# Three matmuls of 256 columns per weight tile in place of one of 512 and one of 256

## The chip, the cores and the metric

The kernel runs on one core of one Trainium2 chip. The metric is device time in microseconds (us) from start to end of one execution; the lower the better. The core has a matrix engine (TensorE, "PE" in the profile, its weight loads "PEld"), a vector engine (VectorE, "DVE"), a scalar engine (ScalarE, "ACT"), GpSimd ("POOL") and a sync engine ("SP") that here issues DMAs. TensorE writes to PSUM, an accumulation memory of eight banks; one bank holds 512 float32 values on each of 128 partitions. Everything else is kept in SBUF, the core's working memory.

## The reference

The reference is a small decoder trunk on 256 tokens of width 2048, with one gated-linear-attention layer and one block-sparse attention layer, each followed by a gated feed-forward layer with a convolution of width 3. Cut to what matters here:

```
h = x
h = h + gla_mixer(h)       # proj = rms_norm(h) @ w_in -> q, k, v, g ; ... ; o @ w_out
h = h + conv_ffn(h)        # a, u = split(conv3(rms_norm(h) @ w_up)); (silu(a) * u) @ w_down
h = h + moba_mixer(h)      # q, k, v projections, 16 heads; softmax; o @ w_out
h = h + conv_ffn(h)
```

All values are float32. FFN_HIDDEN is 5632, so each w_up is 2048 x 11264 and each w_down 5632 x 2048. Most of the work is products of the 256 tokens with these weight matrices.

## The kernel before

The kernel keeps the residual stream `h` feature-major: eight tiles of 128 partitions x (2 x 256), which hold two blocks of 128 features for all 256 tokens. A product whose result is feature-major takes a 128 x 128 tile of weights as the stationary operand and the tokens as the moving one.

The matmuls run in float32r, a type that keeps fewer bits than float32. To come close to float32, each operand is split into a high part (the value cast to float32r) and a low part (the rest). A product is then high x high + high x low + low x high; low x low is left out. The tokens' parts lie side by side in one tile: columns 0 to 255 hold the high part, 256 to 511 the low part.

`gemm` (line 222) makes one feature-major result of 2 x 128 features x 256 tokens over `kts` contraction tiles: 16 for a width of 2048, 44 for the down-projections. A step takes one half chunk of weights, 1024 columns, which is 4 contraction tiles x 2 feature blocks. For each of these eight weight tiles there are two matmuls. Line 233 multiplies the high weights with all 512 columns, so columns 0 to 255 of the result get high x high and 256 to 511 get high x low. Line 234 multiplies the low weights with the first 256 columns and adds that to columns 0 to 255. In the last step of a group all tiles of feature block 0 come before those of block 1. The result fills two banks, and the two halves are still to be added.

That addition is part of the evacuation. `both` (line 257) copies the right half to SBUF on ACT (line 259) and adds the left half on DVE (line 260). It is used for keys, queries, gates and the up-projections, and a multiplication by the token's norm scale follows (lines 395, 464, 479, 506). `residual` (line 266) adds the two halves to `h` one after the other on DVE (lines 267, 268). The last group of the kernel does the same for each feature block separately (lines 675, 676), and then sends the block out.

`gemm_tok` (line 238) makes token-major results (values, and the heads' queries and keys). Here the tokens are stationary and 512 columns of weights are moving; three matmuls (lines 248 to 250) add up in the same columns. The change doesn't touch it, but it shares the PSUM pool `acc_ps`, which has three buffers of two banks; two more banks, in the pool `mis_ps`, serve everything else.

Other runs of 256 columns are in `mix` (lines 316 to 318, three that add up in the same columns, and 319 with 128), in the gate logits (line 353), the scores (589) and the sums over partitions (196).

`WeightStream` loads the weights ahead by DMA and splits each half chunk of 1024 columns on ACT (line 77) and DVE (line 78), two steps ahead, into three buffers each of `whi` and `wlo`. The order of the instructions on each engine comes from a scheduler that works on the program as a whole; `after(n, job)` puts smaller jobs such as norms, scores and softmax between the steps of the big products. Values are scaled (lines 309, 310, 312) when the norm scale is there, the first of them ten steps behind their product.

Of the kernel before, what the change touches and what calls it, by code (L numbers as in the profile page):

```python
# [8 lines left out]
F32 = mybir.dt.float32  # L9
# [9 lines left out]
S = 256  # L19
# [15 lines left out]


class WeightStream:
    """Weights in the order of their use: loaded ahead, split ahead into float32r high and low parts."""

    AHEAD = 2  # L40

# [49 lines left out]
def trunk(ctx: ExitStack, tc: tile.TileContext, xT, cst, msk, w1p, w2a, w_k, w_qa, w_v, w_g, w_go,  # L91
# [7 lines left out]
    parts = ctx.enter_context(tc.tile_pool(name="parts", bufs=3))  # L99
    tmp = ctx.enter_context(tc.tile_pool(name="tmp", bufs=6))  # L100
    small = ctx.enter_context(tc.tile_pool(name="small", bufs=2))
    acc_ps = ctx.enter_context(tc.tile_pool(name="acc_ps", bufs=3, space=PSUM))
    mis_ps = ctx.enter_context(tc.tile_pool(name="mis_ps", bufs=2, space=PSUM))
    dram = ctx.enter_context(tc.tile_pool(name="dram", bufs=1, space=DRAM))

# [3 lines left out]
    def temp(name, shape=(128, 2, S), dt=F32):  # L109
        return tmp.tile(list(shape), dt, name=name, tag="temp")  # L110
# [78 lines left out]
        V.tensor_mul(dst, y, u)  # L189

    def spread_sum(ps, sq):
        """Sum over partitions on every partition; the operand goes in as its two float32r parts."""
        halves_ = temp("sum_parts", dt=F32R)
        split(halves_[:, 0], halves_[:, 1], sq)
        for i in range(2):
            T.matmul(ps, ones, halves_[:, i], start=i == 0, stop=i == 1)
# [25 lines left out]
        return halves_  # L222

    def gemm(xs, kts):
        ps = acc_ps.tile([128, 2, 512], F32, name="acc")
        for q0 in range(0, kts, 4):
            hi, lo = step()
            order = [(k, b) for k in range(4) for b in range(2)]
            for k, b in sorted(order, key=lambda kb: kb[1]) if q0 == kts - 4 else order:
                kt = q0 + k  # L230
                x = xs(kt)
                c = k * 256 + b * 128
                T.matmul(ps[:, b, :], hi[:, c:c + 128], x, start=kt == 0, stop=False)  # L233
                T.matmul(ps[:, b, :S], lo[:, c:c + 128], x[:, :S], start=False, stop=kt == kts - 1)  # L234
        ws.prefetch(cur[0])
        return ps

# [16 lines left out]
    def rows(xs):  # L254
        return lambda kt: xs[kt // 2][:, kt % 2, :]

    def both(ps, name):
        t = temp(name)
        A.copy(t, ps[:, :, S:])
        V.tensor_add(t, t, ps[:, :, :S])  # L260
        return t

    def bc(r):
        return r[:, None, :S].to_broadcast([128, 2, S])

    def residual(ps, p):
        V.tensor_add(h[p], h[p], ps[:, :, S:])
        V.tensor_add(h[p], h[p], ps[:, :, :S])

    def split(dst_hi, dst_lo, src):  # L270
        A.copy(dst_hi, src)
        V.tensor_sub(dst_lo, src, dst_hi.bitcast(F32))

    class Norm:
        """Takes the residual stream pair by pair: norm-weighted operand parts and the token scale."""

        def __init__(self, c, name, columns=False):
            self.c, self.name, self.columns, self.xs = c, name, columns, []
# [9 lines left out]
        def close(self):  # L288
            self.rstd = token_rstd(self.acc, self.columns)

    # GLA
    nrm = Norm(C_GN, "xw", True)
    for p in range(2):
        nrm.operand(p)
# [9 lines left out]
    vg = [(vg0[hd], vg1[hd // 2][:, hd % 2, :]) for hd in range(GH)]  # L304

    def v_out(v, ps, n):
        """Scales the values; the first token tile goes out as float32r parts, the second as it is."""
        r0, r1 = (n.rstd[:, S + t:S + t + 1] for t in range(2))
        A.activation(v[0][:, 0, :], ps[:, 0, :], AF.Copy, scale=r0)
        V.scalar_tensor_tensor(v[0][:, 1, :], ps[:, 0, :], r0, v[0][:, 0, :].bitcast(F32),  # L310
                               op0=OP.mult, op1=OP.subtract)
        A.activation(v[1], ps[:, 1, :], AF.Copy, scale=r1)
# [78 lines left out]
    for hd in range(GH):  # L391
        ps = gemm(xs, KT)
        rstd = nrm.rstd
        k = both(ps, "k")
        V.tensor_mul(k, k, bc(rstd))
        b = bcum[hd]
        d = small.tile([128, 2, 4], F32, name="dec", bufs=4)
        last = chunks(b)[:, :, :, 63:64]
        A.activation(d[:, :, :, None], last, AF.Exp)
        ke = slot([128, 2, 2, 2, 128], F32, "kie")  # L400
        qk = slot([128, 2, 2 * S], F32, "qq")
        eb = temp("eb")
        A.activation(eb, b, AF.Exp, scale=-1.0)
        V.tensor_mul(ke[:, :, :, 0, :], tiles(k), tiles(eb))
        A.copy(ke[:, :, :, 1, 64:], ke[:, :, :, 0, 64:])
        db = temp("db")
        V.tensor_sub(chunks(db), last.to_broadcast([128, 2, 4, 64]), chunks(b))
        A.activation(db, db, AF.Exp)
        V.tensor_mul(ke[:, :, :, 1, :64], tiles(k)[:, :, :, :64], tiles(db)[:, :, :, :64])
        V.tensor_mul(qk[:, :, 384:448], ke[:, :, 0, 1, :64], d[:, :, 1:2].to_broadcast([128, 2, 64]))  # L410
        V.tensor_mul(qk[:, :, 448:512], k[:, :, 64:128], db[:, :, 64:128])
        kie.append(ke)
        qq.append(qk)
        dec.append(d)
# [45 lines left out]

    for hd in range(GH):
        ps = gemm(xs, KT)
        q = both(ps, "q")
        V.scalar_tensor_tensor(q, q, 1.0 / 16.0, bc(rstd), op0=OP.mult, op1=OP.mult)
        eb = temp("eb")
        A.activation(eb, bcum[hd], AF.Exp)
        qk = qq[hd]
        V.tensor_mul(qk[:, :, :S], q, eb)
        A.copy(qk[:, :, 256:320], qk[:, :, 128:192])
        V.tensor_mul(qk[:, :, 320:384], qk[:, :, 192:256], dec[hd][:, :, 2:3].to_broadcast([128, 2, 64]))  # L470
        for lag, job in ((2, gla_scores), (4, gla_values), (6, gla_norm)):
            after(lag, lambda job=job, hd=hd: job(hd))

    go = []
    for hd in range(GH):
        for c in range(2):
            ps = gemm(xs, KT)
            g = both(ps, "g")
            V.tensor_mul(g, g, bc(rstd))
            A.activation(g, g, AF.Silu)  # L480
            V.tensor_mul(g, g, bc(heads[hd]["r"]))
            for i in range(2):
                V.scalar_tensor_tensor(g[:, i, :], heads[hd]["o"][:, 2 * c + i, :], col(C_ON + 2 * c + i),
                                       g[:, i, :], op0=OP.mult, op1=OP.mult)
            gx = slot([128, 2, 2 * S], F32R, "go")
            split(gx[:, :, :S], gx[:, :, S:], g)
            go.append(gx)
# [10 lines left out]
    def ffn(layer, nrm, then):  # L498
        xs = rows(nrm.xs)
        hid = []  # L500
        cw = C_CW + layer * 3 * 2 * FT
        cb = C_CB + layer * 2 * FT
        for j in range(FT):
            ps = gemm(xs, KT)
            t = both(ps, "up")
            V.tensor_mul(t, t, bc(nrm.rstd))  # L506
            au = temp("au")
            for i in range(2):
                n = i * FT + j
                A.activation(au[:, i, :], t[:, i, :], AF.Identity, bias=col(cb + n),  # L510
                             scale=col(cw + 2 * 2 * FT + n))
                V.scalar_tensor_tensor(au[:, i, 1:], t[:, i, :S - 1], col(cw + 2 * FT + n), au[:, i, 1:],  # L512
                                       op0=OP.mult, op1=OP.add)
                V.scalar_tensor_tensor(au[:, i, 2:], t[:, i, :S - 2], col(cw + n), au[:, i, 2:],  # L514
                                       op0=OP.mult, op1=OP.add)
            A.activation(au[:, 0, :], au[:, 0, :], AF.Silu)
            V.tensor_mul(au[:, 0, :], au[:, 0, :], au[:, 1, :])
            if j % 2 == 0:
                hid.append(slot([128, 2, 2 * S], F32R, "hid"))
            split(hid[-1][:, j % 2, :S], hid[-1][:, j % 2, S:], au[:, 0, :])  # L520
        then(rows(hid))
# [3 lines left out]
    n_q = Norm(C_MN, "xw", True)  # L525
    ffn(0, n_ffn, lambda xs: project(xs, FT, [n_q]))

    # cross-decoder: with S equal to the block, no block is fully past, and only the own block counts
    V.scalar_tensor_tensor(kqw, col(C_KN), 128.0 ** -0.5, col(C_QN), op0=OP.mult, op1=OP.mult)
    bias = []  # L530

# [32 lines left out]
        return t_  # L564

    def features(t_, c, f, scale, c0):
        """Turns two heads; queries or keys 0..127 stay whole, those from c0 on go out as float32r parts."""
        tp = bank("tr", (128, 2, S))
        for i in range(2):
            for t in range(2):  # L570
                T.transpose(tp[:, i, 128 * t:128 * t + 128],  # L571
                            t_[:, t, (2 * c + i) * 128:(2 * c + i + 1) * 128], ident)
        whole, halves_ = f[0][:, 2 * c:2 * c + 2, :], f[1][c]
        A.activation(whole, tp[:, :, :128], AF.Copy, scale=scale)
        hi, lo = halves_[:, :, 0, :], halves_[:, :, 1, :]
        A.activation(hi, tp[:, :, c0:], AF.Copy, scale=scale)
        V.scalar_tensor_tensor(lo, tp[:, :, c0:], scale, hi.bitcast(F32), op0=OP.mult, op1=OP.subtract)
# [89 lines left out]
    def last(xs):  # L667
        for p in range(NP):
# [3 lines left out]
                nc.sync.dma_start(out[p], h[p].rearrange("a b c -> a (b c)"))  # L672
                continue
            for i in range(2):
                V.tensor_add(h[p][:, i], h[p][:, i], ps[:, i, S:])
                V.tensor_add(h[p][:, i], h[p][:, i], ps[:, i, :S])
                (nc.sync, A)[i].dma_start(out[p, :, S * i:S * i + S], h[p][:, i])

    ffn(1, n_ffn, last)
# [86 lines left out]
```

## Time and profile before

| | |
|---|---|
| median of 3 runs | 2264.71 us (2260.82 to 2264.79) |
| profiled execution | 2262.2 us of span; the page gives no other time of it |
| instructions | 31304, of which 12514 matmuls and 12514 weight loads |
| PE busy | 2249.8 us (99%) |
| PEld busy | 1945.7 us (86%) |
| DVE busy | 1502.8 us (66%) |
| ACT busy | 1199.6 us (53%) |
| DMA | 420.17 MB, mean 186 GB/s |
| granted TensorE clock | 0.999 |

The span runs from the first to the last instruction of one execution. Busy time of an engine is the time in which at least one of its instructions runs; matmuls overlap in the records, so a TensorE that is 99% busy isn't at its peak, and the mean duration of a matmul is longer than the distance from its start to the next one's. Groups of instructions are listed as line, engine, operation, output<-inputs, shape and count, then busy time in us, mean duration in ns, and the idle time of the engine ahead of them with what ended it. Rows of the timeline begin with the start and the duration in us. The chain of waits is followed back from the last instruction, at each step to what released it.

### The profile page before, as it was taken

The numbers are of one execution on the slowest core, as the hardware profiler recorded it, in microseconds if no ns is written. First come the engines' busy times: TensorE is split into PE (matmuls) and PEld (weight loads), VectorE is DVE, ScalarE is ACT, GpSimd is POOL, SyncE is SP. The second block draws the span as 40 slices with busy tenths as digits, with TensorE's granted clock in tenths as the row PEclk, the third lists the DMA queues.
The fourth block names the chain that finished last, engine by engine and source line by source line (L and its number), as shares of the span: only waits on it lengthen the run. The fifth ranks groups of instructions, "written<-read, shape, count | busy, mean of one in ns | idle before, by whom it ended". The sixth has DMA issues, their size and how long they took to land.

```text
span 2262.2 us, 31304 instructions
## 1 busy us (share of the span) xinstructions
PE 2249.8 (99%) x12514; PEld 1945.7 (86%) x12514; DVE 1502.8 (66%) x2021; ACT 1199.6 (53%) x1667; POOL 25.0 (1%) x27
## 2 busy tenths in 40 slices
PE   8999999999999999999999999999999999999999
PEld 6889888888888888888888888888888888888887
DVE  6676776777777777555556666667777777764444
ACT  6555654655555555444456565556555555543332
POOL 0000000000000000000010000000000000000000
PEclk9999999999999999999999999999999999999999
DMA  6554455555555554555565544555555555555553
GB/s 243 186 186 142 170 185 186 188 195 194 187 186 189 193 195 178 186 199 190 197 219 181 179 168 149 186 186 187 186 186 186 187 186 187 186 183 190 196 205 122
DMA packets 62180, 420.17 MB, mean 186 GB/s; under 512 B 7073, under 2 KB 7857, under 8 KB 13138
## 3 DMA queue, kind: packets, MB, share of 16 engines
q1 hardware_dynamic: 61074, 415.82, 52.3%
q0 software_dynamic: 672, 2.17, 0.3%
q8 instruction: 98, 1.61, 0.3%
q14 instruction: 48, 0.39, 0.1%
q10 hardware_dynamic: 288, 0.18, 0.0%
HBM read 416.02 MB, written 2.12 MB: 185 GB/s over the span
## 4 chain that ended last, share of the span: by engine, by line
PE 99%; DVE 0%; DMA 0%; ACT 0%; SPq 0%; issue 0%
PE acc L233 54%; PE acc L234 27%; PE acc L249 5%; PE acc L250 5%; PE acc L248 5%; PE sT L431 0%; PE tr L571 0%; DMA h<-xT 0%; PE s L589 0%; PE pT L609 0%; DVE bcum L366 0%; PE z L339 0%; PE s L587 0%; PE o L319 0%; PE oT L319 0%; DVE wlo L78 0%
## 5 line engine op out<-in xcount | busy, mean ns | idle before, releaser
L78 DVE TENSOR_TENSOR wlo<-wraw,whi 128x1024 fp32r<-128x1024 f32 (+1 forms) x785 | 959.9, 1224 | 671.3 <-ACT whi L77 665.8
L77 ACT CAST whi<-wraw 128x1024 fp32r<-128x1024 f32 (+1 forms) x785 | 823.7, 1050 | 970.8 <-PE acc L233 744.7
L233 PE MATMUL acc<-xw,whi 128*128 128x512 f32 x3328 | 1166.6, 396 | 0.0
L234 PE MATMUL acc<-xw,wlo 128*128 128x256 f32 x3328 | 929.5, 279 | 0.0
L233 PEld LDWEIGHTS acc<-xw,whi 128*128 128x128 f32 x3328 | 624.7, 188 | 149.8
L234 PEld LDWEIGHTS acc<-xw,wlo 128*128 128x128 f32 x3328 | 627.0, 188 | 0.2
L233 PE MATMUL acc<-hid,whi 128*128 128x512 f32 x1408 | 492.9, 396 | 0.0
L234 PE MATMUL acc<-hid,wlo 128*128 128x256 f32 x1408 | 392.7, 279 | 0.0
L233 PEld LDWEIGHTS acc<-hid,whi 128*128 128x128 f32 x1408 | 264.3, 188 | 63.7
L234 PEld LDWEIGHTS acc<-hid,wlo 128*128 128x128 f32 x1408 | 265.2, 188 | 0.0
L248 PE MATMUL acc<-whi,xw 128*128 128x512 f32 x256 | 101.7, 397 | 6.8 <-ACT xw L166 4.9
L249 PE MATMUL acc<-wlo,xw 128*128 128x512 f32 x256 | 102.0, 398 | 1.0 <-DVE wlo L78 1.0
L250 PE MATMUL acc<-whi,xw 128*128 128x512 f32 x256 | 101.3, 396 | 0.0
L249 PE MATMUL acc<-wlo,xkv 128*128 128x512 f32 x256 | 100.6, 393 | 0.0
L248 PE MATMUL acc<-whi,xkv 128*128 128x512 f32 x256 | 100.5, 393 | 0.0
L250 PE MATMUL acc<-whi,xkv 128*128 128x512 f32 x256 | 100.4, 392 | 0.0
L510 ACT ACTIVATE au<-up,cs 128x256 f32<-128x256 f32 x176 | 95.8, 592 | 5.0 <-DVE up L506 5.0
L233 PE MATMUL acc<-go,whi 128*128 128x512 f32 x256 | 90.5, 399 | 0.0
L233 PE MATMUL acc<-ox,whi 128*128 128x512 f32 x256 | 89.1, 394 | 0.0
L512 DVE SCALAR_TENSOR_TENSOR au<-up,cs,au 128x255 f32<-128x255 f32 x176 | 76.9, 479 | 0.0
L514 DVE SCALAR_TENSOR_TENSOR au<-up,cs,au 128x254 f32<-128x254 f32 x176 | 76.7, 478 | 0.0
L234 PE MATMUL acc<-go,wlo 128*128 128x256 f32 x256 | 71.9, 281 | 0.0
(196 smaller groups left out, 1551.8 us busy)
## 6 DMA issues: line engine op xcount, KB each, us to landing
wraw<-w_up SPq DMA_DIRECT2D x176, 1024.0 KB, 4.7
wraw<-w_dn SPq DMA_DIRECT2D x80, 1024.0 KB, 4.8
wraw<-w_g SPq DMA_DIRECT2D x16, 1024.0 KB, 4.7
wraw<-w_go SPq DMA_DIRECT2D x16, 1024.0 KB, 4.7
wraw<-w_mq SPq DMA_DIRECT2D x16, 1024.0 KB, 4.8
wraw<-w_kk SPq DMA_DIRECT2D x16, 1024.0 KB, 4.7
wraw<-w_kv SPq DMA_DIRECT2D x16, 1024.0 KB, 4.7
wraw<-w_mo SPq DMA_DIRECT2D x16, 1024.0 KB, 4.8
```

The lines of the kernel that those rows point to most:

```text
L77: nc.scalar.copy(hi[:, a:b], src[:, a:b])
L78: nc.vector.tensor_sub(lo[:, a:b], src[:, a:b], hi[:, a:b].bitcast(F32))
L233: T.matmul(ps[:, b, :], hi[:, c:c + 128], x, start=kt == 0, stop=False)
L234: T.matmul(ps[:, b, :S], lo[:, c:c + 128], x[:, :S], start=False, stop=kt == kts - 1)
L248: T.matmul(ps[:, t, :], xh, wh, start=kt == 0, stop=False)
L249: T.matmul(ps[:, t, :], xh, wl, start=False, stop=False)
L250: T.matmul(ps[:, t, :], xl, wh, start=False, stop=kt == KT - 1)
L510: A.activation(au[:, i, :], t[:, i, :], AF.Identity, bias=col(cb + n), scale=col(cw + 2 * 2 * FT + n))
L512: V.scalar_tensor_tensor(au[:, i, 1:], t[:, i, :S - 1], col(cw + 2 * FT + n), au[:, i, 1:], op0=OP.mult, op1=OP.add)
L514: V.scalar_tensor_tensor(au[:, i, 2:], t[:, i, :S - 2], col(cw + n), au[:, i, 2:], op0=OP.mult, op1=OP.add)
```

## The change

Each weight tile now has three matmuls of 256 columns: high weights x high tokens, high weights x low tokens, and low weights x high tokens. All three add up in the same 256 columns of PSUM, so the result of a group fills one bank: feature block 0 in columns 0 to 255, block 1 in 256 to 511. Only the first matmul of the group carries the start flag; the last step's order by feature block is gone. The evacuation reads the finished sum in one instruction: `both` is gone, `residual` is one addition, and the last group has one addition for each feature block instead of two. The feature-major result has its own name in the pool `acc_ps` with two buffers of one bank, and the token-major one has two buffers of two banks instead of three. Some comments and docstrings are taken out too.

```diff
-    acc_ps = ctx.enter_context(tc.tile_pool(name="acc_ps", bufs=3, space=PSUM))
+    acc_ps = ctx.enter_context(tc.tile_pool(name="acc_ps", bufs=2, space=PSUM))
...
     def gemm(xs, kts):
-        ps = acc_ps.tile([128, 2, 512], F32, name="acc")
+        ps = acc_ps.tile([128, 2, S], F32, name="fac", bufs=2)
+        first = True
         for q0 in range(0, kts, 4):
             hi, lo = step()
-            order = [(k, b) for k in range(4) for b in range(2)]
-            for k, b in sorted(order, key=lambda kb: kb[1]) if q0 == kts - 4 else order:
+            for k in range(4):
                 kt = q0 + k
                 x = xs(kt)
-                c = k * 256 + b * 128
-                T.matmul(ps[:, b, :], hi[:, c:c + 128], x, start=kt == 0, stop=False)
-                T.matmul(ps[:, b, :S], lo[:, c:c + 128], x[:, :S], start=False, stop=kt == kts - 1)
+                for b in range(2):
+                    c = k * 256 + b * 128
+                    for w, a in ((hi, 0), (hi, S), (lo, 0)):
+                        T.matmul(ps[:, b, :], w[:, c:c + 128], x[:, a:a + S], start=first,
+                                 stop=kt == kts - 1 and w is lo, skip_group_check=True)
+                        first = False
...
-    def both(ps, name):
-        t = temp(name)
-        A.copy(t, ps[:, :, S:])
-        V.tensor_add(t, t, ps[:, :, :S])
-        return t
...
     def residual(ps, p):
-        V.tensor_add(h[p], h[p], ps[:, :, S:])
-        V.tensor_add(h[p], h[p], ps[:, :, :S])
+        V.tensor_add(h[p], h[p], ps)
...
-        k = both(ps, "k")
-        V.tensor_mul(k, k, bc(rstd))
+        k = temp("k")
+        V.tensor_mul(k, ps, bc(rstd))
...
-            t = both(ps, "up")
-            V.tensor_mul(t, t, bc(nrm.rstd))
+            t = temp("up")
+            V.tensor_mul(t, ps, bc(nrm.rstd))
...
             for i in range(2):
-                V.tensor_add(h[p][:, i], h[p][:, i], ps[:, i, S:])
-                V.tensor_add(h[p][:, i], h[p][:, i], ps[:, i, :S])
+                V.tensor_add(h[p][:, i], h[p][:, i], ps[:, i])
```

Queries and gates are changed as the keys are.

More of the change, by code (lines that the diff above doesn't have):

```diff
@@ L462, in trunk @@
         ps = gemm(xs, KT)
-        q = both(ps, "q")
-        V.scalar_tensor_tensor(q, q, 1.0 / 16.0, bc(rstd), op0=OP.mult, op1=OP.mult)
+        q = temp("q")
+        V.scalar_tensor_tensor(q, ps, 1.0 / 16.0, bc(rstd), op0=OP.mult, op1=OP.mult)
         eb = temp("eb")
@@ L477, in trunk @@
             ps = gemm(xs, KT)
-            g = both(ps, "g")
-            V.tensor_mul(g, g, bc(rstd))
+            g = temp("g")
+            V.tensor_mul(g, ps, bc(rstd))
             A.activation(g, g, AF.Silu)
```

## The prediction

> **What bounds the kernel now.** I read the page's first and fourth parts first, then the chain of waits with its shares to a tenth, then the groups by line.
>
> ```profile
> span 2262.2 us, 31304 instructions
> PE 2249.8 (99%) x12514; PEld 1945.7 (86%) x12514; DVE 1502.8 (66%) x2021; ACT 1199.6 (53%) x1667; POOL 25.0 (1%) x27
> ...
> by line: PE acc L233 54.1%; PE acc L234 27.2%; PE acc L249 5.0%; PE acc L250 5.0%; PE acc L248 5.0%; PE sT L431 0.4%; PE tr L571 0.3%; DMA h<-xT 0.3%; PE s L589 0.3%; PE pT L609 0.2%; DVE bcum L366 0.2%; PE z L339 0.2%; PE s L587 0.2%; PE o
> ...
> L77 ACT CAST whi<-wraw 128x1024 fp32r<-128x1024 f32 (+1 forms) x785 | 823.7, 1050 | 970.8 <-PE acc L233 744.7
> L233 PE MATMUL acc<-xw,whi 128*128 128x512 f32 x3328 | 1166.6, 396 | 0.0
> L234 PE MATMUL acc<-xw,wlo 128*128 128x256 f32 x3328 | 929.5, 279 | 0.0
> L233 PEld LDWEIGHTS acc<-xw,whi 128*128 128x128 f32 x3328 | 624.7, 188 | 149.8
> L233 PE MATMUL acc<-hid,whi 128*128 128x512 f32 x1408 | 492.9, 396 | 0.0
> L233 PE MATMUL acc<-go,whi 128*128 128x512 f32 x256 | 90.5, 399 | 0.0
> L233 PE MATMUL acc<-ox,whi 128*128 128x512 f32 x256 | 89.1, 394 | 0.0
> ```
>
> TensorE ends everything. Lines 233 and 234, the two matmuls that the change replaces, hold 81.3% of the chain, 1839 us of the span. The idle column of line 233 is 0.0: it never waits for the weight split, the DMAs or a PSUM buffer. ACT, on the other hand, waits 745 us for TensorE to free weight buffers. The counts give 3328 + 1408 + 256 + 256 = 5248 pairs, so a pair costs 1839 / 5248 = 350.4 ns: 233.2 for the 512 columns (54.1%) and 117.2 for the 256 (27.2%).
>
> The mean of one instruction (396, 279 and 188 ns) isn't that cost, since instructions overlap. What counts is from one start to the next; here is the timeline, and then the number of line 233's instructions in two stretches.
>
> ```profile
> 1000.33 0.40 PE L233 MATMUL acc<-hid,whi 128*128 128x512 f32 x1
> 1000.33 0.19 PEld L234 LDWEIGHTS acc<-hid,wlo 128*128 128x128 f32 x1
> 1000.56 0.28 PE L234 MATMUL acc<-hid,wlo 128*128 128x256 f32 x1
> ...
> 1000.67 0.39 PE L233 MATMUL acc<-hid,whi 128*128 128x512 f32 x1
> ```
>
> ```profile
> core 0: us, PE busy (x) PEld busy (x), PEclk, DMA share, GB/s
> 450.00:850.00 400.00, 400.00 (x1155) 216.38 (x1154) 1.00 0.55 190
> 1550.00:2000.00 450.00, 450.00 (x1275) 239.31 (x1274) 1.00 0.53 186
> ```
>
> The next weights load while a matmul streams. Pairs keep one of two rhythms at the same granted clock: 400 / 1155 = 346.3 ns in the first stretch, 450 / 1275 = 352.9 in the second. Both are up-projections, with the same code and buffers. What sets the rhythm the trace doesn't say; the mean of 350.4 is a mixture.
>
> **The change, part by part.**
>
> *The matmuls.* The columns streamed stay 768 per weight tile: 512 + 256 before, 3 x 256 after. What is added is a third matmul with its own weight load, 5248 of each. So the question is what a 256-column matmul costs behind another one. Elsewhere in the kernel such runs exist, in the same float32r type; the first fence is the value stage, the second the gate logits, the third a place among line 233's own pairs.
>
> ```profile
> 1396.97 0.39 PE L249 MATMUL acc<-wlo,xkv 128*128 128x512 f32 x1
> 1397.20 0.39 PE L250 MATMUL acc<-whi,xkv 128*128 128x512 f32 x1
> 1397.43 0.39 PE L248 MATMUL acc<-whi,xkv 128*128 128x512 f32 x1
> 1397.65 0.28 PE L316 MATMUL o<-p,vm 128*128 128x256 f32 x1
> 1397.77 0.28 PE L317 MATMUL o<-p,vm 128*128 128x256 f32 x1
> ...
> 1398.25 0.28 PE L318 MATMUL o<-p,vm 128*128 128x256 f32 x1
> 1398.37 0.40 PE L249 MATMUL acc<-wlo,xkv 128*128 128x512 f32 x1
> ```
>
> ```profile
> 65.88 0.64 PE L353 MATMUL gk<-zst,w2t 81*128 81x256 f32 x4
> 66.36 0.40 PE L249 MATMUL acc<-wlo,xw 128*128 128x512 f32 x1
> ```
>
> ```profile
> 178.43 0.40 PE L316 MATMUL oT<-attr,vg 128*128 128x256 f32 x2
> 178.67 0.28 PE L234 MATMUL acc<-xw,wlo 128*128 128x256 f32 x1
> 178.78 0.28 PE L317 MATMUL oT<-attr,vg 128*128 128x256 f32 x1
> 178.90 0.28 PE L318 MATMUL oT<-attr,vg 128*128 128x256 f32 x1
> 179.02 0.38 PE L319 MATMUL oT<-att,vg 128*128 128x128 f32 x2
> ```
>
> In the value stage 512-column matmuls follow each other at (1397.65 - 1396.97) / 3 = 227 ns. Then five starts of 256 columns, from 1397.77 to 1398.37, are 120 ns apart. The four gate matmuls take 0.48 / 4 = 120 ns each. In the third run five take 0.59 / 5 = 118. Halving the columns from 227 to 120 saves 107 and not 113: each matmul carries about 13 ns beside its columns (2 x 120 - 227), and 227 + 120 = 347 is just the quicker rhythm of line 233's pairs. A third matmul should thus add one such share to that rhythm: 3 x 120 = 360 ns for a weight tile. Lines 316 to 318 add up in the same PSUM columns one behind the other, as the new code does, and that shows no extra cost.
>
> The bounds: as cheap as the quickest slot of line 234, from 1000.56 to 1000.67 and so some 115 ns with the rounding, 3 x 115 = 345; as dear as the slower rhythm laid on top, 360 + (352.9 - 346.3) = 366.6. I take 360, because two of the three runs show 120 and the quicker rhythm is the sum of 227 and 120.
>
> Cost: (360 - 350.4) x 5248 = +50.4 us. Bounds: (345 - 350.4) x 5248 = -28 and (366.6 - 350.4) x 5248 = +85 us.
>
> The Trainium skill, "TensorE: Matmul & The Clock Gate", section "Back-to-back issue gap", gives the spacing as N/2.4 + 2.5 ns, so a fixed share of only 2.5 ns a matmul. That too speaks against the change, at 5248 x 2.5 = +13 us as an estimate, some 2277 us in all. This trace doesn't agree: by that rule 512 columns would take 216 ns and 256 would take 109, where the rows have 227 and 120.
>
> *The evacuation.* It loses ACT's copy and DVE's addition 104 times (by the loops 4 keys, 4 queries, 8 gates, 88 up-projections), one of two DVE additions for 31 residuals, and two of four short additions at the end.
>
> ```profile
> L259 ACT COPY up<-acc x88: 567/581/584, 411.4 to 2009.7; 128x512 f32<-128x512 f32 x88
> L260 DVE TENSOR_TENSOR up<-up,acc x88: 679/681/689, 412.0 to 2011.0; 128x512 f32<-128x512 f32 x88
> L268 DVE TENSOR_TENSOR h<-h,acc x31: 683/686/689, 319.6 to 2227.2; 128x512 f32<-128x512 f32 x31
> ```
>
> ACT gets 104 x 0.581 = 60 us back and DVE 104 x 0.681 + 31 x 0.686 = 92 us. I cost both at nothing: line 233 never waited for them, so TensorE can't start anything sooner. That a lighter DVE might speed TensorE through less memory traffic I exclude as well: the stretch 450 to 850 us is full of this work and runs the quicker rhythm. Weights are needed later, at 2.88 us a step (8 x 360) instead of 2.80, so the split and the DMAs gain slack.
>
> *PSUM.* The feature-major products now have two buffers of one bank, the token-major ones two of two banks instead of three. A feature-major group lasts at least 32 x 345 ns = 11 us, and the one before it is evacuated within that by a single instruction of 0.7 us: nothing. The tight place is the start, where values are scaled late.
>
> ```profile
> 60.22 0.39 PE L248 MATMUL acc<-whi,xw 128*128 128x512 f32 x1
> ...
> L312 ACT ACTIVATE vg<-acc,rstd_h x4: 676/682/686, 43.5 to 109.2; 128x512 f32<-128x512 f32 x4
> ```
>
> The third group starts at 60.2 us and will need the first group's buffer, whose last read begins at 43.5 and lasts 0.7. So 16 us cover it; without that cover it would cost what the read is late, once.
>
> *The tail.* Only the two halves' final additions are on the path.
>
> ```profile
> 2257.60 0.42 DVE L675 TENSOR_TENSOR h<-h,acc 128x256 f32<-128x256 f32 x1 [6.29 <-PE acc L234]
> ...
> 2258.84 0.42 DVE L676 TENSOR_TENSOR h<-h,acc 128x256 f32<-128x256 f32 x1
> 2259.30 0.35 ACTq L677 DMA_DIRECT2D out_dram<-h  x1
> ```
>
> Four follow the last matmul, two are left: -2 x 0.42 = -0.8 us. The two that are left are not spread over the last step any more than before, since these too stood behind the last matmul.
>
> **Sum.** 2262.2 + 50.4 - 0.8 = 2311.8 us of span. The page has no other time of its execution; the median of the three runs is 2264.7, 2.5 above the span, and I carry that over: 2314 us, +2.2%.
>
> **The rivals.**
>
> *The shorter rhythm.* All tiles keep the third run's 118 ns, or the 117.2 that line 234 has on the chain: 354 or 351.6, so +18.9 or +6.3 us, less 0.8: 2283 or 2270 us. For it: that run lies among line 233's own pairs. Against it: five matmuls are too few to show a rhythm that lasts, and two other runs have 120. A mixture of 118 and 120 lies between, around 2299. The spacing rule of the Trainium skill quoted above would land in this case, at its 2277.
>
> *Faster.* The place is the slot behind a 256-column matmul; the price is 115 ns in all three, 2262.2 - 28 - 0.8 + 2.5 = 2236 us. It decides from 350.4 / 3 = 116.8 ns a matmul downwards. For it: pairs in the quicker rhythm do show this slot. Against it: the 512-column neighbour takes 233 and not 227 there, so the short slot borrows from the long one, and no run of 256 columns holds it.
>
> *The change does less than it says.* The two matmuls with the high weights load the same tile twice in a row; were the second load dropped, the pair would act like one of 512 columns: 346.3 x 5248, -21.5 us, 2242. Against it: lines 248 and 249 take the same stationary tile and the page counts as many loads as matmuls, 12514. It is counted with the faster case.
>
> *A dearer rhythm.* One more of the 6.6 ns steps on every tile, 366.6: 2349 us. For it: 352.9 does show such a step on top of the plain sum for whole stages. Loads and matmuls now come every 60 ns instead of 350.4 / 4 = 88, and no long stretch of the trace shows that pace.
>
> **How the numbers follow.** 120 ns: 0.45, and its own range is 2304 to 2324 (119.5 to 120.5, and the run's scatter). Shorter rhythm and mixtures: 0.28. Dearer: 0.12, and 0.05 for still more. Faster, both ways: 0.10. A measurement of this kernel can tell 0.2%, or 4.5 us, from no change; of the shorter rhythm only its cheapest end reaches that, 0.04. So slower 0.86, same 0.04, faster 0.10. The range of 2268 to 2350 takes in the shorter and the dearer rhythm and leaves out the faster case and what is dearer still.
>
> **What would show it.** In the new profile the matmul's line should have 15744 instructions, TensorE and its loads 17762 each. In 400 us of an up-projection 400 / 0.120 = 3333 of them say that the sum is right, 3390 that 118 holds, over 3425 that the change gains. Idle before the matmul's line should stay 0.0 and ACT's wait for TensorE should grow. The prediction is wrong if the spacing is not near 120 ns, or if TensorE begins to wait for a buffer.

## The result and the profile after

The changed kernel takes 2318.94 us (median of 4 runs, 2318.54 to 2319.68) against 2263.46 before: a ratio of 1.0246, 95% interval 1.0233 to 1.0258. Forecast were 2314 us, within 2268 to 2350, and slower.

The first lines of the page after the change, the chain's shares to a tenth, two groups by line, and the number of the matmul line's instructions in the two stretches in which line 233 was counted before:

```profile
span 2317.1 us, 41573 instructions
PE 2302.3 (99%) x17762; PEld 2235.2 (96%) x17762; DVE 1424.9 (61%) x1884; ACT 1147.6 (50%) x1563; POOL 26.2 (1%) x27
...
by line: PE fac L236 81.5%; PE acc L253 4.9%; PE acc L254 4.9%; PE acc L252 4.9%; PE sT L428 0.4%; PE tr L568 0.3%; DMA h<-xT 0.3%; PE s L586 0.2%; PE pT L606 0.2%; DVE bcum L363 0.2%; PE z L336 0.2%; PE oT L316 0.2%; PE o L316 0.2%; DVE wl
...
L77 ACT CAST whi<-wraw 128x1024 fp32r<-128x1024 f32 (+1 forms) x785 | 821.9, 1048 | 1105.1 <-PE fac L236 953.3
L236 PE MATMUL fac<-xw,whi 128*128 128x256 f32 x6656 | 1199.2, 283 | 0.0
L236 PEld LDWEIGHTS fac<-xw,whi 128*128 128x128 f32 x6656 | 1038.3, 192 | 0.1
```

```profile
450.00:850.00 400.00, 400.00 (x3336) 400.00 (x3335) 1.00 0.52 184
1550.00:2000.00 450.00, 450.00 (x3751) 449.91 (x3750) 1.00 0.52 183
```

TensorE still ends everything, and DVE and ACT have become lighter, as the page's busy times show, without any gain. ACT's wait for TensorE, 745 us before, is 953. Line 236 holds 81.5% of 2317.1 us, 1888 us; over 15744 instructions that is 120 ns each, 360 for a weight tile instead of 350.4. Both stretches give it alike: 400 / 3336 and 450 / 3751 are 120 ns. (A count takes in two or three matmuls that began just before its stretch.) The two rhythms of the kernel before are gone.

The matmul line thus brings 1888 - 1839 = 49 of the 54.9 us that the span grew by; the shares are rounded to 0.1%, 2.3 us. The starts in the trace give the whole: the feature-major stages grew by 51.4 us, the token-major stage between them by 3.7 and the beginning by 0.7, and the tail is 0.9 shorter. So a second, small part lies in the token-major stage. Its first matmul and the first one behind the stage start here, before and after:

```profile
1127.56 0.39 PE L248 MATMUL acc<-whi,xw 128*128 128x512 f32 x1
...
1419.85 0.39 PE L233 MATMUL acc<-ox,whi 128*128 128x512 f32 x1
```

```profile
1162.19 0.40 PE L252 MATMUL acc<-whi,xw 128*128 128x512 f32 x1
...
1458.17 0.40 PE L236 MATMUL fac<-ox,whi 128*128 128x256 f32 x2
```

It lasted 292.3 us and now lasts 296.0, though none of its matmuls was touched. The list of waits names new ones in it, 2.5 us in all, and the timeline shows the place; the kernel before follows behind it:

```profile
PE s L584 <- ACT p L612: 1.2, 1, 1.2
...
PE pT L606 <- DVE st L593: 0.7, 1, 0.7
PE acc L252 <- ACT k L553: 0.4, 1, 0.4
PE acc L252 <- ACT vm L309: 0.2, 1, 0.2
```

```profile
1403.85 0.55 PE L606 MATMUL pT<-mk,s 128*128 128x128 f32 x3 [0.74 <-DVE st L593]
1405.62 0.49 PE L584 MATMUL s<-k,q 128*128 128x128 f32 x2 [1.22 <-ACT p L612]
1405.86 0.60 PE L586 MATMUL s<-k,q 128*128 128x256 f32 x3
1406.70 0.50 PE L252 MATMUL acc<-whi,xkv 128*128 128x512 f32 x1 [0.24 <-ACT vm L309]
```

```profile
1366.93 0.60 PE L589 MATMUL s<-k,q 128*128 128x256 f32 x3
1367.37 0.40 PE L248 MATMUL acc<-whi,xkv 128*128 128x512 f32 x1
...
1371.46 0.27 PE L609 MATMUL pT<-mk,s 128*128 128x128 f32 x1
```

After the change, TensorE works through steps of the softmax with nothing of the big products between them: from 1402.05 to 1406.70 us, 4.65 us, no big matmul starts, and the next one waits for `vm`, the reading of a token-major result (line 309). Before, 18 big matmuls run between the scores (line 589) and the next step (line 609), and in the softmax no such stretch is longer than some 1.5 us. The first matmul starts at 5.7 instead of 4.9 us, and waits for the same as before, `xw` of ACT.

### The profile page after: what moved, and what is told of

Same layout as the page of the kernel before. It is cut to its first block, busy times and chain, and to the rows that moved or that the text cites. A ratio compares the mean times of both kernels' runs of the same rounds, so it can differ in the third digit from the quotient of the medians.

```text
span 2317.1 us, 41573 instructions
## 1 busy us (share of the span) xinstructions
PE 2302.3 (99%) x17762; PEld 2235.2 (96%) x17762; DVE 1424.9 (61%) x1884; ACT 1147.6 (50%) x1563; POOL 26.2 (1%) x27
## 4 chain that ended last, share of the span: by engine, by line
PE 99%; DVE 0%; ACT 0%; DMA 0%; SPq 0%; issue 0%; DVEq 0%
PE fac L236 82%; PE acc L253 5%; PE acc L254 5%; PE acc L252 5%; PE sT L428 0%; PE tr L568 0%; DMA h<-xT 0%; PE s L586 0%; PE pT L606 0%; DVE bcum L363 0%; PE z L336 0%; PE oT L316 0%; PE o L316 0%; DVE wlo L78 0%; PE s L584 0%
## 5 line engine op out<-in xcount | busy, mean ns | idle before, releaser
L236 PE MATMUL fac<-xw,whi 128*128 128x256 f32 x6656 | 1199.2, 283 | 0.0
L236 PEld LDWEIGHTS fac<-xw,whi 128*128 128x128 f32 x6656 | 1038.3, 192 | 0.1
L236 PE MATMUL fac<-xw,wlo 128*128 128x256 f32 x3328 | 941.9, 283 | 0.0
L236 PEld LDWEIGHTS fac<-xw,wlo 128*128 128x128 f32 x3328 | 638.8, 192 | 0.0
L236 PE MATMUL fac<-hid,whi 128*128 128x256 f32 x2816 | 507.0, 283 | 0.0
L236 PEld LDWEIGHTS fac<-hid,whi 128*128 128x128 f32 x2816 | 439.3, 192 | 0.0
L236 PE MATMUL fac<-hid,wlo 128*128 128x256 f32 x1408 | 398.5, 283 | 0.0
L236 PEld LDWEIGHTS fac<-hid,wlo 128*128 128x128 f32 x1408 | 270.3, 192 | 0.0
L236 PE MATMUL fac<-ox,whi 128*128 128x256 f32 x512 | 92.6, 283 | 0.0
L236 PE MATMUL fac<-go,whi 128*128 128x256 f32 x512 | 92.2, 283 | 0.0
```

The lines of the kernel that those rows point to most:

```text
L236: T.matmul(ps[:, b, :], w[:, c:c + 128], x[:, a:a + S], start=first, stop=kt == kts - 1 and w is lo, skip_group_check=True)
```

## The experiments

### The parts, one at a time

**The third matmul alone**, in the kernel before with its buffers and its evacuation:

```diff
-                T.matmul(ps[:, b, :], hi[:, c:c + 128], x, ...)
+                T.matmul(ps[:, b, :S], hi[:, c:c + 128], x[:, :S], ...)
+                T.matmul(ps[:, b, S:], hi[:, c:c + 128], x[:, S:], ...)
                 T.matmul(ps[:, b, :S], lo[:, c:c + 128], x[:, :S], ...)
```

> The kernel before, with only the 512-column matmul cut into two of 256 into the same two halves of PSUM: buffers, order and evacuation stay as they were. Theory (the third matmul and its load are the whole loss): 3 x 120 = 360 ns for a weight tile, 2263 + 50 = about 2313 us, ratio 1.022; the changed kernel was at 2319. Rival (part of the loss comes from adding up in the same columns, or from the smaller PSUM pools): 3 matmuls at 117 to 118 ns, 2268 to 2285 us, ratio 1.002 to 1.010.

2314.71 us, ratio 1.0230 (1.0213 to 1.0247). The count of line 233, now one in three of the matmuls:

```profile
450.00:850.00 400.00, 314.49 (x1112) 213.36 (x1112) 1.00 0.52 183
1550.00:2000.00 450.00, 353.69 (x1250) 239.82 (x1250) 1.00 0.51 183
```

400 / 1112 and 450 / 1250 are 360 ns for a weight tile. Nearly the whole loss is the third matmul with its load. Adding up in the same columns costs nothing more: by the starts in the trace each feature-major stage takes as long here as in the changed kernel, for instance 507.1 us for either up-projection. The token-major stage, with three buffers as before, takes 292.3 us (1159.17 to 1451.46), as in the kernel before.

**The evacuation alone**: the kernel before, whose evacuation reads one half and adds nothing.

```diff
-        t = temp(name)
-        A.copy(t, ps[:, :, S:])
-        V.tensor_add(t, t, ps[:, :, :S])
-        return t
+        return ps[:, :, :S]
```

> The kernel before, with its matmuls and buffers as they were and only the evacuation of the changed kernel: it reads one half of the result and adds nothing, so the product with the tokens' low parts, in the other half, is left out. Theory (the evacuation is wholly behind TensorE): 2262 us less 0.8 at the tail, ratio 0.999 to 1.000, pairs at 350 ns. Rival (fewer ACT and DVE instructions help or hurt TensorE): a ratio below 0.997, or above 1.003 if the new order of the small jobs makes TensorE wait, as for 2.3 us in the softmax of the changed kernel.

2263.14 us, ratio 1.0001 (0.9992 to 1.0011). `residual` and the last group lose their second addition in the same way, and the changed multiplications read the result itself. The evacuation is worth nothing: TensorE's waits are those of the kernel before, all in the first 93 us and for the tokens' and the weights' parts.

**The smaller pool alone**:

```diff
-    acc_ps = ctx.enter_context(tc.tile_pool(name="acc_ps", bufs=3, space=PSUM))
+    acc_ps = ctx.enter_context(tc.tile_pool(name="acc_ps", bufs=2, space=PSUM))
```

> The kernel before with two buffers instead of three in the accumulation pool, so feature-major and token-major results share two; nothing else is changed and nothing is left out. Theory (the pools cost nothing by themselves): ratio 0.999 to 1.001. Rival (the smaller pool, by making TensorE wait or by moving the small jobs of the softmax, gives the 4 us that the changed kernel has above the third matmul alone): ratio 1.0015 to 1.003, with TensorE waiting for ACT or DVE in the softmax.

2273.30 us, ratio 1.0042 (1.0025 to 1.0059). This is the rival's side, and above its range of 1.0015 to 1.003. The waits of TensorE:

```profile
PE acc L233 <- DVE g L260: 3.3, 1, 3.3
...
PE s L587 <- ACT p L615: 1.2, 1, 1.2
...
PE pT L609 <- DVE st L596: 0.7, 1, 0.7
PE acc L248 <- ACT k L556: 0.4, 1, 0.4
PE acc L248 <- ACT vm L312: 0.2, 1, 0.2
```

The last four are, one for one, the waits of the changed kernel's softmax: two token-major buffers instead of three bring them, as only the number of buffers differs here. The wait of 3.3 us in the gates comes from feature-major results that share these two buffers here, and the changed kernel, where they have their own, doesn't have it. After the same break in the big matmuls TensorE's clock also fell for a moment (0.55 granted from 1377 to 1380 us), which the profile of the changed kernel doesn't show. With it the token-major stage takes 297.6 us here, 5.3 more than before.

### What the share beside the columns is

Half the columns take more than half the time, 120 against 227 ns. These runs ask what the rest, some 13 ns of each matmul, belongs to. Each leaves out products, so only the spacings count, and each is a single run.

**Fewer columns.** The changed kernel with `x[:, a:a + m]` and `ps[:, b, :m]`, where `m` differs by stage. The last two stages came out the other way round than the expectation says: the second up-projection had 64 columns and the last down-projection all 256.

> The changed kernel with fewer moving columns in all contraction tiles but the first, another number in each stage: 248 for keys, 240 queries, 232 gates, 224 attention output, 192 first up, 160 first down, 128 second output, 256 second up (unchanged), 64 last down. The left-out columns are tokens whose products are left out. Theory (a fixed share of 13 ns beside N/2.4): 116.7, 113.3, 110 ns for the first three, and then a floor near the 111 to 112 ns at which 64-column matmuls follow each other in the scores of the kernel before. Rival (the load of 128 columns of float32r weights itself takes 120 ns): 120 ns in every stage.

Counts of the matmul line, in order: 248 columns, 232, 224, 192, 64, and 256 again.

```profile
110.00:145.00 35.00, 35.00 (x306) 35.00 (x305) 1.00 0.53 189
...
215.00:290.00 75.00, 70.99 (x627) 70.73 (x628) 1.00 0.51 182
310.00:390.00 80.00, 80.00 (x715) 80.00 (x715) 1.00 0.55 198
450.00:850.00 400.00, 400.00 (x3569) 400.00 (x3567) 1.00 0.55 196
...
1600.00:2300.00 700.00, 700.00 (x3283) 700.00 (x3282) 0.50 0.29 103
2400.00:2600.00 200.00, 200.00 (x1669) 200.00 (x1668) 1.00 0.55 194
```

One in 16 of the contraction tiles still has all columns in these counts. 256 columns take 200 / 1669 = 120 ns. By the starts in the trace 248 take 115, 232 take 113, and 224 and 192 take 112, the same for both; the stages with 160 and 128 columns give 112, too. So there is a floor of some 112 ns with a load of 128 float32r columns for each matmul, and 256 columns lie 8 ns above it: the rival, that the load itself takes 120, is out. That the floor is the load itself is not shown: no run here has few columns beside small loads. The stage with 64 columns did something not looked for: 5 us into it the granted clock went down to 0.50, for 894 us, and a matmul took 213 ns, nearly twice the floor. This made the run 2638.97 us long.

**Smaller loads**, in the changed kernel, with `w[:r, c:c + m]` for the weights, `x[:r, ...]` for the tokens and `ps[:m, ...]` for the result:

> The changed kernel with smaller stationary tiles in all contraction tiles but the first: low weights with 64 of 128 columns for keys, queries and gates; all weights with 64 columns in the attention output and first up-projection; 64 of 128 rows in the first down-projection; all with 32 columns in the second output; low weights with 32 columns in the second up; last down unchanged. The products of the columns and rows not loaded are left out. Theory (the share of 13 ns belongs to the matmul, whatever is loaded): 120 ns everywhere. Rival (the share is what a weight load takes from the matmul beside it): with half the columns loaded 113 ns, with a quarter 110, and in the stages where only the low tile is small one spacing in three drops by 7 to 10 ns; 64 rows change nothing.

2272.83 us. Counts: the low loads alone with 64 columns, then all loads with 64 columns, then 64 of the 128 rows, then the low loads with 32 columns, then unchanged.

```profile
110.00:150.00 40.00, 40.00 (x345) 40.00 (x344) 1.00 0.53 187
...
450.00:850.00 400.00, 400.00 (x3517) 400.00 (x3516) 1.00 0.55 193
950.00:1100.00 150.00, 150.00 (x1237) 148.66 (x1237) 1.00 0.51 183
1600.00:2000.00 400.00, 400.00 (x3394) 392.43 (x3394) 1.00 0.53 187
2100.00:2250.00 150.00, 150.00 (x1253) 150.00 (x1252) 1.00 0.55 195
```

400 / 3517 is 113.7 ns (113.4 without the first contraction tile, from the starts in the trace), against 120 at the end. With 64 rows 1185 of 1234 spacings stayed at 120. So the share depends on how many columns are loaded and not on the rows; the theory, that it belongs to the matmul whatever is loaded, fell. A load of fewer columns also gives a result of fewer partitions here, and these runs can't tell the two apart. And a quarter of the low load gave 118, less of a gain than a half with 117 (starts in the first stretch). How the spacing goes with the size of the load:

> The changed kernel with fewer columns in all weight loads of whole stages, but for the first contraction tile: 96 of 128 in the first up-projection, 64 in the first down, 112 in the second up, 32 in the last down; elsewhere unchanged. The features not loaded are left out. Theory (the time a load takes from the matmul beside it grows with its columns, 13.3 ns for 128): 116.7, 113.3, 118.3 and 110 ns. Rival (it only has the two values seen so far): 120 for 112 and 96 columns, 113.4 for 64 and 32.

```profile
450.00:850.00 400.00, 400.00 (x3447) 400.00 (x3446) 1.00 0.54 189
950.00:1100.00 150.00, 150.00 (x1324) 150.00 (x1322) 1.00 0.55 194
1600.00:2000.00 400.00, 400.00 (x3518) 400.00 (x3517) 1.00 0.55 193
2100.00:2230.00 130.00, 130.00 (x1127) 121.66 (x1126) 1.00 0.56 198
```

96, 64, 112 and 32 columns: 116.0, 113.3, 113.7 and 115.4 ns, the first contraction tiles with all 128 columns among them; the run took 2254.43 us. Both expectations fell: any smaller load is quicker than 120, but not in proportion to its size, and 112 columns are quicker than 96. What costs the 8 ns stays open.

### The two rhythms, and a quicker kernel

**Grouped**: the kernel before, with the eight 512-column matmuls of a step first.

```diff
-            for k, b in sorted(order, key=lambda kb: kb[1]) if q0 == kts - 4 else order:
...
+            for k, b in order:
...
+                T.matmul(ps[:, b, :], hi[:, c:c + 128], xs(q0 + k), start=q0 + k == 0, stop=False)
+            for k, b in order:
+                c = k * 256 + b * 128
+                T.matmul(ps[:, b, :S], lo[:, c:c + 128], xs(q0 + k)[:, :S], start=False,
+                         stop=q0 + k == kts - 1)
```

The last step's order by feature block goes with it.

> The kernel before, with the eight matmuls of 512 columns of a step first and the eight of 256 columns behind them; nothing is left out. Theory (each matmul costs N/2.4 + 13 ns, and the slower rhythm of the kernel before comes from taking 512 and 256 columns in turn): steady spacings of 227 and 120 ns, so 347 ns for a weight tile instead of 350.4, and 2263 - 5248 x 0.0034 = about 2245 us, ratio 0.992. Rival (the slower rhythm belongs to the stage or the buffers): the mean stays at 350 and the time at 2263, ratio 1.000.

2259.05 us, ratio 0.9986 (0.9977 to 0.9995), near the rival's 1.000 and not the theory's 0.992. But the two rhythms are gone: the starts in the trace give 349.2 ns for a weight tile in both up-projections, where the kernel before has 346.7 and 353.3. The timeline has a step of it, and then one of the next kernel, **longer runs**, in which every second step takes its low weights first:

```diff
+            for job, part in ((high, hi), (low, lo)) if n % 2 == 0 or q0 == 0 else ((low, lo), (high, hi)):
+                job(q0, part)
```

> The grouped kernel with every second step turned round (low weights first), so that runs are 16 matmuls long and only half as many changes between 512 and 256 columns are left; nothing is left out. Theory (in the grouped kernel the 512-column matmuls behind a change take up to 236 ns and come down to 227 after five, some 19 ns lost for each change): 346.7 + 19/16 = 347.9 ns for a weight tile, 13 us less than before, ratio 0.994. Rival (the long 512-column spacings belong to the position in the step and not to the change): 349.1 ns as in the grouped kernel, ratio 0.9986.

```profile
600.42 2.00 PE L231 MATMUL acc<-xw,whi 128*128 128x512 f32 x8
602.26 1.11 PE L234 MATMUL acc<-xw,wlo 128*128 128x256 f32 x8
603.21 0.63 PE L231 MATMUL acc<-xw,whi 128*128 128x512 f32 x2
```

```profile
500.35 2.08 PE L235 MATMUL acc<-xw,wlo 128*128 128x256 f32 x16
...
502.26 3.82 PE L229 MATMUL acc<-xw,whi 128*128 128x512 f32 x16
...
505.92 2.08 PE L235 MATMUL acc<-xw,wlo 128*128 128x256 f32 x16
```

In runs of eight the 512 columns take 1.84 / 8 = 230 ns, in runs of sixteen 3.66 / 16 = 228.8, and 227 where nothing else comes between. By the starts, the five matmuls of 512 columns behind a change take 27 ns more in all, and the first two of 256 columns behind one 7 to 8 less, so that a change to 512 columns and back costs some 20 ns. The second kernel has 347.9 ns for a weight tile in both up-projections, just as expected, and 2252.75 us, ratio 0.9962 (0.9947 to 0.9976).

**Low weights in bfloat16**, in turn, grouped and in longer runs. They meet the upper half-words of the high token parts, so nothing has to be computed for it; this product is then less exact, by how much is not on record.

```diff
+            if low is BF16:
+                lo = lo.bitcast(BF16)[:, :1024]
...
+                xb = xs(q0 + k)[:, :S].bitcast(BF16).rearrange("p (n t) -> p n t", t=2)[:, :, 1]
+                T.matmul(ps[:, b, :S], lo[:, c:c + 128], xb, ...)
```

> The same bfloat16 low weights, but with 512 and 256 columns in turn as in the kernel before. Nothing is left out. Theory (the load takes its share from the matmul beside it): the small load now lies beside the 512 columns, which take 213 to 220 ns, and the float32r load beside the 256 columns, which keep about 120: 333 to 340 ns for a weight tile, 2175 to 2210 us, ratio 0.961 to 0.977. Rival (share of the matmul): 350 ns, ratio 1.000.

> The kernel with all 512-column matmuls of a step first, and with the low weights of the feature-major products kept as bfloat16; they meet the upper half-words of the high token parts, read in place. Nothing is left out. Theory, formed after the smaller loads (a float32r load of 128 columns takes some 13 ns from the matmul beside it, and a bfloat16 load takes less, down to nothing): a spacing of 107 to 113 ns between the 256-column matmuls instead of 119, the 512-column ones as in the grouped kernel at 230.6, together 338 to 343 ns for a weight tile against 349, so 2200 to 2228 us, ratio 0.973 to 0.985. Rival (the 13 ns belong to every matmul, whatever its load): 349 ns and 2259 us, ratio 0.999.

> The same order with bfloat16 low weights; nothing is left out. In the grouped kernel with such weights a step took 2773 ns, 346.6 a weight tile, and its 512-column matmuls stayed near 232 ns to the end of the run. Theory (they too would come down to 227 in a longer run, and a change costs some 20 ns): about 343 ns, 2230 us, ratio 0.985. Rival (they stay at 232): 346 ns, 2243 us, ratio 0.991.

In turn they take 2327.48 us, ratio 1.0288 (1.0273 to 1.0304), and neither side of the expectation was right. The timeline of that kernel:

```profile
600.13 0.48 PE L236 MATMUL acc<-xw,whi 128*128 128x512 f32 x1
600.45 0.10 PEld L238 LDWEIGHTS <-wlo 128*128 128x128 bf16 x1 [0.16 <-issue]
600.45 0.29 PE L238 MATMUL acc<-xw,wlo 128*128 128x256 bf16 x1
600.45 0.20 PEld L236 LDWEIGHTS acc<-xw,whi 128*128 128x128 f32 x1
600.49 0.48 PE L236 MATMUL acc<-xw,whi 128*128 128x512 f32 x1
```

The bfloat16 load is not taken early beside the float32r matmul. It starts 0.32 us behind that matmul's start, where a float32r load starts with it, and a weight tile takes 600.49 - 600.13 = 0.36 us. Grouped, the type changes only between runs of eight: 2246.36 us, ratio 0.9926 (0.9910 to 0.9943), between the theory's 0.973 to 0.985 and the rival's 0.999. In longer runs 2231.39 us, ratio 0.9868 (0.9852 to 0.9885), close to the theory's 2230 us and 0.985, with this count of line 234:

```profile
450.00:850.00 400.00, 284.51 (x1163) 212.68 (x1162) 1.00 0.55 192
```

400 / 1163 is 344 ns for a weight tile. This kernel is the quickest here. By the starts in it, its runs of 256 columns settle at 113.3 ns, with loads of all 128 columns and results of all 128 partitions: the 8 ns above the floor are gone with the bfloat16 load, as the theory of the grouped kernel had it, though the moving operand changes its type as well. The 512 columns come down to 227 only after ten matmuls, and a change of type and back costs some 60 ns (5500 ns for 16 weight tiles against 16 x 340), not 20. That the total came out as expected is thus in part luck.

## Why the prediction was right, and where not

- *The bound and the third matmul.* Right in mechanism and size. 120 ns was taken from two runs of four and five matmuls, and it lasts: of 15724 spacings within the line 15645 are 120 ns. The sum said +50.4 us; the chain shows +49, the starts of the stages +51.4. The third matmul alone gives a ratio of 1.0230, the whole change 1.0246.
- *The shorter rhythm.* Fell. The run at 118 ns lay among pairs of 512 and 256 columns, and a long run of 256 knows no rhythm at all. That 227 and 120 add up to the quicker rhythm was luck: by the starts its two spacings are 231.7 and 115.0 ns. Both rhythms belong to taking two lengths in turn, since both go when these are grouped; which of the two a stage keeps stays open.
- *Faster, or a load that drops out.* Fell: loads and matmuls are 17762 each, and 115 ns appeared in no long run of full tiles. *The dearer rhythm* didn't come either.
- *"Each matmul carries about 13 ns beside its columns".* As a number it held, since the 120 and 227 ns that it was worked out from came again. As a property of the matmul it didn't, since with 64 or 112 columns loaded 256 columns take some 113 ns.
- *The spacing rule.* The rule of the Trainium skill that the prediction set against the rows ("TensorE: Matmul & The Clock Gate", "Back-to-back issue gap", where it is the gap of an isolated matmul) would have given +2.5 ns a weight tile, as an estimate. The trace doesn't agree: measured are +9.6.
- *The evacuation at nothing.* Right: 1.0001 by itself. The cover, a TensorE that doesn't wait for it, was still there.
- *The PSUM buffers at nothing.* Wrong. "The tight place is the start" looked at the right kind of cover and at the wrong stage: at the start there were no new waits; in the softmax, where the third token-major buffer had let big matmuls run between the small jobs, TensorE now waits. By the prediction's own sign, "if TensorE begins to wait for a buffer", this part failed. The token-major stage takes 3.7 us more in the changed kernel, and that is most of what the forecast lacks (2317.1 of span against 2311.8).
- *The tail.* Right. The two additions that are left stand behind the last matmul, at 2313.06 us, and the span ends 4.0 us behind it instead of 4.9:

```profile
2313.06 0.28 PE L236 MATMUL fac<-hid,wlo 128*128 128x256 f32 x1
2313.38 0.75 DVE L672 TENSOR_TENSOR h<-h,fac 128x256 f32<-128x256 f32 x2 [6.45 <-PE fac L236]
```

## What to carry to other kernels

Where TensorE ends everything, count matmuls and loads and not columns alone: the spacing from start to start, for the same type and length in a steady run, times the count, gave this change to 5 us, and work taken from engines that nobody waits for gave nothing. A pool that is made smaller has to be looked at in every stage that shares it. Runs of equal matmuls are cheaper than lengths or types taken in turn, and with long runs a cheaper, less exact type for the low parts paid: 2231 us.

## What was not expected of the hardware

- With 64 moving columns beside loads of 128 the granted clock went to 0.50 for nearly the whole stage, though the records show TensorE and its loads busy all the time (700.00 of 700 us); in the stages with 128 columns or more it stayed up. This is one run.
- A bfloat16 load behind a float32r matmul isn't taken early: 362 ns for a weight tile instead of 350.
- A 256-column matmul takes 120 ns with 128 float32r weight columns, but some 113 with 112 and 116 with 96. Why, no run here shows.
